# Ten projection slabs formed by token and turned by transposes, and the first half's end moved behind the second half's inverses

## The chip, the cores and the metric

The kernel runs on one core of one Trainium2 chip, as one launch. The metric is the device time of that launch in microseconds (us). Three runs of the kernel before gave 1227.54, 1227.72 and 1228.52; the median is 1227.72. TensorE (PE) does the matmuls, and its weight loads are listed apart as PEld; VectorE is DVE, ScalarE is ACT, GpSimd is POOL and SyncE is SP. Each engine takes its instructions strictly in the order in which they stand in the program.

## What is computed

One decoder layer on x of 256 tokens by 2048 channels, all in float32. Cut to what matters here:

```
u = rms_norm(x) * norm1_g                       # 256 x 2048
q, k, v, z = split(u @ w_in)                    # 3 x 1024 columns, then 3360 for z
z = z + (previous token's z - z) * shift_mix
r, k7, v7, w_lo, a_lo, g_lo = split(z)          # 3 x 1024 columns, then 288
attn = 16 heads of windowed attention on q, k, v
rw   = 16 heads of a delta-rule recurrence over the 256 tokens (r, k7, v7, decay from w_lo,
       rate from a_lo), then a norm per head, a bonus, and a gate from g_lo
h   = x + concat(attn, rw) @ w_out
out = rms_norm(h + (silu(gate) * up) @ w_down), gate, up = rms_norm(h) @ w_gate_up
```

## The kernel before

Every matmul against a big weight is made of three products of two-part numbers. A weight piece is split into `wh` (ACT copies it at reduced precision, line 148) and `wl` (DVE takes the rest, line 149), the activations likewise (`u1h`, `u1l`), and each output gets high x high, high x low and low x high. Weights come by SP's queue in pieces of 512 KB, three buffers deep, and six split pieces may stand ahead of PE. So ACT and DVE work about six pieces ahead, and in their order the other work stands between pieces.

The layer is worked in this order. A start normalises x and forms the 288 narrow columns (`lo`). Then `projections` goes through two halves of 512 channels (8 heads each), and in each half through six slabs of 512 columns: k7, r, v7 (tiles `zk`, `zr`, `zv`), then v, q, k of attention (`v`, `qT`, `kT`). Then come the product with w_out (slabs `p` and `o`), the two FFN products (`ga`, `gb`, `up`, then `d`), and the final norm.

Two ways of forming a slab exist. `slab` makes it by token: the tokens are the stationary operand, the weights stream through, 512 columns an instruction, 6 instructions for each of 16 chunks of the inner dimension. `slab_T` makes it by channel: the weights are stationary and the 256 tokens stream through, so an instruction has 256 columns, and a slab takes two passes with 96 instructions each. In the kernel before only v goes by `slab` in the projections; the other five of each half go by `slab_T`, since the later steps want channels on the partitions. The token's normalising factor then lies along the free axis, so it is laid out once over all partitions as `rbc1` (`along_tokens`, lines 263 to 270), and DVE multiplies every 128x256 block by it (lines 483 and 923).

Beside these main slabs runs side work: the recurrence of a half and its attention. It is written as generators that `run` and `step` (lines 203 to 233) mix in: after each piece of a main slab up to two side steps are issued if their due time has come, in units of a simple clock (`now`), and a generator that yields "wait" is passed over. That alone sets the order of the side instructions; nothing is reordered by time on the chip.

For each half the recurrence needs the inverse of a triangular 64x64 block per head and chunk. Its 32x32 corners (`T1`, lines 726 to 740) are found by 31 dependent steps on DVE. Then T1 and a rearranged copy of it (`U1`, a copy by ACT, line 757, in the buffer `e9`) go to DRAM and come back in another layout as `T` and `U64` (lines 755 to 771, all DMAs on ACT's queue). PE then forms the missing corner with `T` (`C0h`), then with `U64` (`C1h`), line 775 on. The recurrence proper follows (`Zh`, `Xh`, `Hh`, `Yh`), and its output `y` also lies in `e9`. At the end of a half (`end`, lines 863 to 903) y is normalised, turned by eight transposes (`tyh`, line 892), scaled and gated into `mix`. The first half's `end` runs as soon as the second half has passed `products.add` (line 725), which is ahead of the second half's 31 steps. `U1` of the second half has to wait until the first half's `y` in the same buffer is read.

The product with w_out takes four groups of channels in the order `OORD`: groups 0 and 1 are attention of the two halves, groups 2 and 3 the recurrence of the two halves. The first two groups in that order are needed by slabs `p` and `o` right after the projections.

Of the kernel before, what the change touches and what calls it, by code (L numbers as in the profile page):

```python
# [16 lines left out]
P = 128  # L17
SEQ = 256
# [57 lines left out]
def layer(ctx: ExitStack, tc: tile.TileContext, I, out, dbg=None, upto=99):  # L76
# [27 lines left out]
    rstd2 = const.tile([P, 2], F32, tag="rstd2", name="rstd2")  # L104
    rstd3 = const.tile([P, 2], F32, tag="rstd3", name="rstd3")
    mhalf = const.tile([P, 2], F32, tag="mhalf", name="mhalf")
    rbc1 = const.tile([P, SEQ], F32, tag="rbc1", name="rbc1")
    DVE.memset(mhalf, -0.5)
    DVE.memset(eps[:, 0:1], GN_EPS)
    DVE.memset(eps[:, 1:2], 1e-24)  # L110
# [42 lines left out]
    def plan_slab(w_ap, kcs, col, n, keep=None):  # L153
        g = 4 if n == 256 else 2
        for g0 in range(0, len(kcs), g):
            plan.append((w_ap, kcs[g0:g0 + g], col, n, keep))

    def take(w_ap, kc, col, units=1):
        key = (w_ap.tensor.name, kc, col)
        while wq[0] < len(plan) and (key not in made or wq[0] * 2 < wq[1] + AHEAD):  # L160
            make(wq[0])
            wq[0] += 1
        wq[1] += units
        return made.pop(key)
# [4 lines left out]
    def slab(ps, w_ap, kcs, col, n, lhs, begin=True, end=True, held=None, tokens=(0, 1)):  # L169

        for i, kc in enumerate(kcs):
# [7 lines left out]
                PE.matmul(o, ah[:, sl], lo[:, :n], start=False, stop=False)  # L179
                PE.matmul(o, al[:, sl], hi[:, :n], start=False, stop=fin)  # L180
            yield

    def slab_T(ps, w_ap, col):

        for kc in range(NK):
            hi, lo = take(w_ap, kc, col, 0.5)
            uh_, ul_ = ulhs(kc)
            for b in range(2):
                cb = slice(b * P, (b + 1) * P)
                o = ps[b][:, 0:SEQ]  # L190
                PE.matmul(o, hi[:, cb], uh_, start=kc == 0, stop=False)  # L191
                PE.matmul(o, hi[:, cb], ul_, start=False, stop=False)  # L192
                PE.matmul(o, lo[:, cb], uh_, start=False, stop=kc == NK - 1)  # L193
            if kc % 2:
                yield

# [124 lines left out]
    for half in range(2):  # L323
        for blks in ((4, 3, 5), (2, 0, 1)):
            for blk in blks:
                col = blk * AW + half * 512
                for c in (col,) if blk == 2 else (col, col + 256):
                    plan_slab(w_in, allk, c, 512 if blk == 2 else 256)
    grp = lambda gs: [k for g in gs for k in range(4 * g, 4 * g + 4)]
    for sl in (2, 3, 0, 1):  # L330
        plan_slab(w_out, grp(OORD[:2]), sl * 512, 512)
# [22 lines left out]
    with tc.tile_pool(name="startp", bufs=1) as st:  # L354
# [57 lines left out]
                ACT.activation(sqj, x_sb[:, t, q * 512:(q + 1) * 512], AF.Square, accum_out=acc[:, t, q:q + 1])  # L412
        DVE.tensor_reduce(accs1, acc, axis=AX.X, op=ALU.add)
        rms_scale(rstd1, accs1)
        along_tokens(rbc1, rstd1, st)
        for t in range(2):

            z = st.tile([P, 480], F32, tag="zlo", name=f"zlo{t}", bufs=2)
# [45 lines left out]

    rp = head_pools.enter_context(tc.tile_pool(name="rp", bufs=1, reuse_waits="tile"))

    def rwkv(half):
        hb = half * 4
        H = f"h{half}"

        def e(i, name, dt=F32):
            return rp.tile([P, 4, SEQ], dt, tag=f"e{i}", name=f"{name}_{H}")

        Z = {}

        def zin(pool, tag, which, name):
            dst = pool.tile([P, 4, SEQ], F32, tag=tag, name=f"{name}_{H}")
            for q in range(2):
                ps = banks(f"{name}{H}{q}")
                yield from slab_T(ps, w_in, RB + which * RW + half * 512 + q * 256)  # L480
                for j in range(2):
                    z = zp.tile([P, SEQ], F32, tag="ztok", name=f"z_{name}{H}{q}{j}", bufs=2)
                    DVE.tensor_tensor(z, ps[j][:, 0:SEQ], rbc1, op=ALU.mult)
                    c = which * 8 + hb + 2 * q + j
                    shift_mix(dst[:, 2 * q + j, :], z, P, V_MIX + c, c)
            Z[name] = dst

        def inputs():
            tags = ((rp, "e2"), (rp, "e1"), (rp, "e3")) if half == 0 else ((act_p, "mx3"), (act_p, "mx1"), (rp, "zvb"))
            for (pool, tag), (which, name) in zip(tags, ((1, "zk"), (0, "zr"), (2, "zv"))):  # L490
                yield from zin(pool, tag, which, name)

        return inputs, rwkv_side(half, hb, H, e, Z)

    def rwkv_side(half, hb, H, e, Z):
# [120 lines left out]
        def core():  # L616
# [97 lines left out]
            for cp in range(2):  # L714
# [7 lines left out]
                    nu = flat(e(6, "nu"))  # L722
                    ACT.dma_start(nu, d1.rearrange("u (s t) -> u s t", t=32))
                yield
            products.add(half)
            T1 = flat(e(3, "T1"))
            POOL.memset(T1, 0.0)
            POOL.memset(T1.rearrange("p a b -> p (a b)")[:, 0::33], 1.0)
# [5 lines left out]
            for t in range(31):  # L734
                a, b = 31 - t, t + 1
                w = tmp[:, 0:a * b].rearrange("p (a b) -> p a b", b=b)
                DVE.tensor_tensor(w, bc(nu[:, t, t + 1:32].unsqueeze(2), [HD, a, b]),
                                  bc(T1[:, t, 0:b].unsqueeze(1), [HD, a, b]), op=ALU.mult)
                DVE.tensor_tensor(T1[:, t + 1:32, 0:b], T1[:, t + 1:32, 0:b], w, op=ALU.add)
                if t % 3 == 2:  # L740
                    yield SUB
                if t == 17:

                    for cp in range(2):
                        pt = opsum(f"AV{H}{cp}")
                        for h in range(8):
                            for c2 in range(2):
                                kr = half_of(1 - c2)
                                PE.matmul(pt[half_of(c2), h * HD:(h + 1) * HD], abk[kr, 2 * cp + c2, h, 0:HD],
                                          vv[cp][kr, c2, h, :], start=True, stop=True,  # L750
                                          tile_position=(64 * (1 - c2), 64 * c2))
                        ACT.copy(av[:, 8 * cp:8 * cp + 8, :], pt.rearrange("p (u i) -> p u i", i=HD))
                    yield
            yield LAT[1]
            ACT.dma_start(d2[0], T1.rearrange("p s t -> p (s t)"))
            U1 = flat(e(9, "U1"))
# [106 lines left out]
        def end():  # L863
            y, bonus = Z["y"], Z["bonus"]
            if half == 1:
                yield from need("gate")
            else:
                while 1 not in products:
                    yield "wait"

            for cp in range(2):
# [35 lines left out]
    def att_inputs(half, Z):  # L907
        A = f"b{half}"
        for i, nm in ((2, "v"), (0, "qT"), (1, "kT")):
            col = i * AW + half * 512  # L910
            if nm == "v":
                ps = banks(f"v{A}")
                yield from slab(ps, w_in, allk, col, 512, ulhs)
                z = Z[nm] = zp.tile([P, 2, 512], F32, tag="atv", name=f"v{A}")
                for t in range(2):
                    ACT.activation(z[:, t, :], ps[t], AF.Copy, scale=rstd1[:, t:t + 1])
            else:
                z = Z[nm] = rp.tile([P, 4, SEQ], F32, tag=nm, name=f"{nm}{A}")
                for q in range(2):
                    ps = banks(f"{nm}{A}{q}")  # L920
                    yield from slab_T(ps, w_in, col + q * 256)
                    for j in range(2):
                        DVE.tensor_tensor(z[:, 2 * q + j, :], ps[j][:, 0:SEQ], rbc1, op=ALU.mult)

    def attention(quad, Z):

        A = f"a{quad}"
        v, qT, kT = Z["v"], Z["qT"], Z["kT"]
        h0 = quad * 4
        bias = rp.tile([P, 4, 256], F32, tag="bias", name=f"bias{A}")  # L930
# [96 lines left out]
            DVE.tensor_tensor(ml[g][:, o, :], mixt[g][:, o, :], mh[g][:, o, :].bitcast(F32), op=ALU.subtract)  # L1027

    mlhs = pair(mh, ml)
    rw, at, done, products = [], [], set(), set()  # L1030
    run(projections())


# [165 lines left out]
KEEP = 8  # L1199
LAT = (6, 5, 2, 6, 5, 3)  # L1200
BS = 1.0
WARM = 8
SUB = 1.5
SIDE_US, MAIN_US, DELAY, EL = 0.9, 1.3, 0.5, 1.5
OORD = (2, 0, 3, 1)


# [22 lines left out]
```

## Time and profile before

| what | value |
|---|---|
| median of three runs | 1227.72 us |
| the profiled execution | 1225.73 us, its span 1224.0 us |
| PE busy | 1204.0 us, 98% of the span |
| DVE busy | 819.0 us, 67% |
| ACT busy | 693.6 us, 57% |
| start | 0 to 29 us |
| projections, ten `slab_T` and two `slab` | 29 to 364 us |
| product with w_out | 369 to 486 us |
| FFN and the rest | 486 to 1224 us |

The span runs from the first instruction to the last; the execution's time has 1.7 us more around it. A matmul's row in the trace is longer than its turn on PE, since matmuls overlap: what a matmul costs is the distance from its start to the next one's start. An idle time in brackets at a row's end says how long the engine waited and for whom.

### The profile page before, as it was taken

What the parts mean: (1) busy time and instruction counts of PE and PEld (TensorE: products, weight loads), DVE (VectorE), ACT (ScalarE), POOL (GpSimd) and SP (SyncE); (2) the same over time, 40 slices, a digit from 0 to 9 for tenths busy, and PEclk for the clock granted to TensorE, in tenths of its full rate; (3) what the DMA queues carried; (4) which work ended last, traced back from release to release, by engine and by line L of the source; (5) the groups of instructions that cost most, each with busy time, mean ns of one, the idle gap of its engine ahead of it and who ended that gap; (6) DMA issues with size and microseconds to landing.
All of it is one profiled execution on the core that took longest, in us unless ns stands there. A gap on an engine that the chain in (4) does not pass through costs nothing.

```text
span 1224.0 us, 21228 instructions
## 1 busy us (share of the span) xinstructions
PE 1204.0 (98%) x7932; PEld 1057.0 (86%) x7932; DVE 819.0 (67%) x1563; ACT 693.6 (57%) x1332; POOL 39.5 (3%) x64
## 2 busy tenths in 40 slices
PE   8999999999999999999999999999999999999997
PEld 7999998898997788888888888888888888888885
DVE  5887786697877757666667566576566655565653
ACT  7875556674557556555555555565555545454543
POOL 4000000000100000000000000000000000010100
PEclk9999999999999999999999999999999999999999
DMA  8656565356674467666666666666666666666664
GB/s 245 197 167 187 155 193 161 96 167 170 177 193 139 132 175 224 201 193 189 190 190 190 190 189 190 190 189 190 189 190 190 192 195 190 195 190 199 184 202 138
DMA packets 148472, 224.05 MB, mean 183 GB/s; under 512 B 18396, under 2 KB 65760, under 8 KB 148368
## 3 DMA queue, kind: packets, MB, share of 16 engines
q1 hardware_dynamic: 132176, 211.12, 58.6%
q10 hardware_dynamic: 13920, 6.06, 1.9%
q0 software_dynamic: 2272, 5.50, 1.4%
q8 instruction: 62, 1.02, 0.4%
q14 instruction: 42, 0.34, 0.1%
HBM read 218.96 MB, written 3.69 MB: 182 GB/s over the span
## 4 chain that ended last, share of the span: by engine, by line
PE 94%; DMA 2%; ACT 1%; DVE 1%; issue 1%; SPq 0%; POOLq 0%; POOL 0%; ACTq 0%; DVEq 0%
PE up L1107 13%; PE ga L1107 7%; PE gb L1107 7%; PE up L1108 7%; PE d L180 6%; PE d L179 6%; PE d L178 6%; PE gb L1108 3%; PE ga L1108 3%; PE o L179 2%; PE o L180 2%; PE o L178 2%; PE qTb L191 1%; PE vb L178 1%; PE zvh L193 1%; PE zvh L192 1%
## 5 line engine op out<-in xcount | busy, mean ns | idle before, releaser
L149 DVE TENSOR_TENSOR wl<-wr,wh 128x512 fp32r<-128x512 f32 (+1 forms) x792 | 541.8, 691 | 346.7 <-ACT wh L148 329.8
L148 ACT ACTIVATE wh<-wr 128x512 fp32r<-128x512 f32 (+1 forms) x792 | 492.5, 627 | 460.4 <-DVE wl L149 245.6
L1107 PE MATMUL up<-u,wh 128*128 128x512 f32 x704 | 244.6, 394 | 0.0
L1108 PE MATMUL up<-u,wl 128*128 128x256 f32 x704 | 195.0, 277 | 0.0
L1107 PEld LDWEIGHTS up<-u,wh 128*128 128x128 f32 x704 | 132.0, 188 | 30.7
L1108 PEld LDWEIGHTS up<-u,wl 128*128 128x128 f32 x704 | 132.1, 188 | 0.0
L178 PE MATMUL d<-wh,hh 128*128 128x512 f32 x336 | 130.7, 389 | 0.0
L180 PE MATMUL d<-wh,hl 128*128 128x512 f32 x336 | 130.7, 389 | 0.0
L179 PE MATMUL d<-wl,hh 128*128 128x512 f32 x336 | 130.7, 389 | 0.0
L1107 PE MATMUL gb<-u,wh 128*128 128x512 f32 x352 | 130.1, 394 | 0.0
L1107 PE MATMUL ga<-u,wh 128*128 128x512 f32 x352 | 129.9, 393 | 0.0
L1108 PE MATMUL gb<-u,wl 128*128 128x256 f32 x352 | 97.6, 277 | 0.0
L1108 PE MATMUL ga<-u,wl 128*128 128x256 f32 x352 | 97.6, 277 | 0.0
L1107 PEld LDWEIGHTS ga<-u,wh 128*128 128x128 f32 x352 | 66.0, 187 | 15.3
L1107 PEld LDWEIGHTS gb<-u,wh 128*128 128x128 f32 x352 | 66.0, 187 | 15.2
L179 PEld LDWEIGHTS d<-wl,hh 128*128 128x128 f32 x336 | 63.1, 188 | 13.2
L178 PEld LDWEIGHTS d<-wh,hh 128*128 128x128 f32 x336 | 63.1, 188 | 13.1
L180 PEld LDWEIGHTS d<-wh,hl 128*128 128x128 f32 x336 | 63.1, 188 | 13.0
L1108 PEld LDWEIGHTS ga<-u,wl 128*128 128x128 f32 x352 | 66.1, 188 | 0.1
L1108 PEld LDWEIGHTS gb<-u,wl 128*128 128x128 f32 x352 | 66.1, 188 | 0.0
L178 PE MATMUL o<-wh,mixh 128*128 128x512 f32 x96 | 37.7, 393 | 0.0
L179 PE MATMUL o<-wl,mixh 128*128 128x512 f32 x96 | 37.6, 391 | 0.0
(340 smaller groups left out, 2050.3 us busy)
## 6 DMA issues: line engine op xcount, KB each, us to landing
wr<-in_w_gate_up_dram SPq DMA_DIRECT2D x176, 512.0 KB, 3.7
wr<-in_w_in_dram SPq DMA_DIRECT2D x96, 512.0 KB, 3.8
wr<-in_w_down_dram SPq DMA_DIRECT2D x88, 512.0 KB, 4.5
wr<-in_w_out_dram SPq DMA_DIRECT2D x32, 512.0 KB, 3.9
wr<-in_w_in_dram SPq DMA_DIRECT2D x8, 288.0 KB, 5.2
x_sb<-in_x_dram SPq DMA_DIRECT2D x8, 256.0 KB, 6.8
biasa<-rvd ACTq DMA_DIRECT2D x4, 512.0 KB, 4.0
xs<-in_x_dram POOLq DMA_DIRECT2D x4, 512.0 KB, 5.5
```

The lines of the kernel that those rows point to most:

```text
L148: ACT.activation(hi[:, :, :n], src, AF.Copy)
L149: DVE.tensor_tensor(lo[:, :, :n], src, hi[:, :, :n].bitcast(F32), op=ALU.subtract)
L178: PE.matmul(o, ah[:, sl], hi[:, :n], start=first, stop=False)
L179: PE.matmul(o, ah[:, sl], lo[:, :n], start=False, stop=False)
L180: PE.matmul(o, al[:, sl], hi[:, :n], start=False, stop=fin)
L191: PE.matmul(o, hi[:, cb], uh_, start=kc == 0, stop=False)
L192: PE.matmul(o, hi[:, cb], ul_, start=False, stop=False)
L193: PE.matmul(o, lo[:, cb], uh_, start=False, stop=kc == NK - 1)
L1107: PE.matmul(ps[b], hi[:, cb], u, start=kc == 0, stop=False)
L1108: PE.matmul(ps[b][:, 0:SEQ], lo[:, cb], u[:, 0, :], start=False, stop=kc == NK - 1)
```

## The change

Three things. First, the five `slab_T` slabs of each half are formed by token too, as `v` is: 96 instructions of 512 columns. ACT copies both token halves out of PSUM with the token's factor as its per-partition scale (new function `by_channel`), so `rbc1` and the DVE multiplies go. A side generator `turn`, due 1.5 units of the clock later, turns the slab by eight 128x128 transposes in two groups of four. For r, k7 and v7 the shift mix then reads the turned block in PSUM as it read the DVE product before; for q and k ACT copies it to SBUF. Attention waits until `kT` is there. Second, the first half's `end` waits for the second half's inverse steps to be done (`solved`, set after line 753) and no longer only for its products. Third, `OORD` is (0, 2, 3, 1) in place of (2, 0, 3, 1), so that slab `p` begins with group 0. Weight pieces of 256 columns no longer occur; the bytes loaded are the same.

```diff
-    rbc1 = const.tile([P, SEQ], F32, tag="rbc1", name="rbc1")
...
-    def slab_T(ps, w_ap, col):
...
-                for c in (col,) if blk == 2 else (col, col + 256):
-                    plan_slab(w_in, allk, c, 512 if blk == 2 else 256)
+                plan_slab(w_in, allk, col, 512)
...
-        along_tokens(rbc1, rstd1, st)
...
+    def by_channel(name, col, use, end):
+        ps = banks(name)
+        yield from slab(ps, w_in, allk, col, 512, ulhs)
+        z = zp.tile([P, 2, 512], F32, tag="ztok", name=f"zt_{name}")
+        for t in range(2):
+            ACT.activation(z[:, t, :], ps[t], AF.Copy, scale=rstd1[:, t:t + 1])
+
+        def turn():
+            yield TURN
+            for q in range(2):
+                pt = opsum(f"zt{name}{q}")
+                for j in range(2):
+                    for t in range(2):
+                        c = (2 * q + j) * P
+                        PE.transpose(pt[:, j * 256 + t * P:j * 256 + (t + 1) * P], z[:, t, c:c + P], ident)
+                use(q, pt)
+                if q == 1:
+                    end()
+                yield
+        side.append(turn())
...
-            for q in range(2):
-                ps = banks(f"{name}{H}{q}")
-                yield from slab_T(ps, w_in, RB + which * RW + half * 512 + q * 256)
+            def use(q, pt):
                 for j in range(2):
-                    z = zp.tile([P, SEQ], F32, tag="ztok", name=f"z_{name}{H}{q}{j}", bufs=2)
-                    DVE.tensor_tensor(z, ps[j][:, 0:SEQ], rbc1, op=ALU.mult)
                     c = which * 8 + hb + 2 * q + j
-                    shift_mix(dst[:, 2 * q + j, :], z, P, V_MIX + c, c)
-            Z[name] = dst
+                    shift_mix(dst[:, 2 * q + j, :], pt[:, j * 256:(j + 1) * 256], P, V_MIX + c, c)
+            yield from by_channel(f"{name}{H}", RB + which * RW + half * 512, use, lambda: Z.update({name: dst}))
...
-            products.add(half)
...
+            solved.add(half)
             yield LAT[1]
             ACT.dma_start(d2[0], T1.rearrange("p s t -> p (s t)"))
...
-                while 1 not in products:
+                while 1 not in solved:
                     yield "wait"
...
-                        DVE.tensor_tensor(z[:, 2 * q + j, :], ps[j][:, 0:SEQ], rbc1, op=ALU.mult)
+                def use(q, pt, z=z):
+                    ACT.copy(z[:, 2 * q:2 * q + 2, :].rearrange("p a t -> p (a t)"), pt)
+                yield from by_channel(f"{nm}{A}", col, use, lambda nm=nm, z=z: Z.update({nm: z}))
...
+        while "kT" not in Z:
+            yield "wait"
...
-OORD = (2, 0, 3, 1)
+OORD = (0, 2, 3, 1)
```

The order in which the instructions stand, at three places. On PE, in the second half, around the end of the slab `zr` (tiles `zrh`) and the start of `zv` (`zvh`); before:

```order
L191 MATMUL zrh_1_3456<-u1h_91,wh_1_3469 128x256
L192 MATMUL zrh_1_3456<-u1l_95,wh_1_3469 128x256
L193 MATMUL zrh_1_3456<-u1h_91,wl_1_3470 128x256
L191 MATMUL zvh_0_3628<-u1h_88,wh_0_3513 128x256
L192 MATMUL zvh_0_3628<-u1l_92,wh_0_3513 128x256
L193 MATMUL zvh_0_3628<-u1h_88,wl_0_3514 128x256
L191 MATMUL zvh_1_3629<-u1h_88,wh_0_3513 128x256
```

After, from the tenth matmul of `zv` on (`ztzrh` are the transposes of the copied slab `zt_zrh`):

```order
L177 MATMUL zvh_1_2953<-wh_1_2887,u1h_87 128x512
L178 MATMUL zvh_1_2953<-wl_1_2888,u1h_87 128x512
L179 MATMUL zvh_1_2953<-wh_1_2887,u1l_91 128x512
L466 MATMUL ztzrh_2981<-ident,zt_zrh_2948 128x128 x4
L177 MATMUL zvh_0_2952<-wh_0_2909,u1h_87 128x512
L178 MATMUL zvh_0_2952<-wl_0_2910,u1h_87 128x512
L179 MATMUL zvh_0_2952<-wh_0_2909,u1l_91 128x512
L177 MATMUL zvh_1_2953<-wh_0_2909,u1h_87 128x512
L178 MATMUL zvh_1_2953<-wl_0_2910,u1h_87 128x512
L179 MATMUL zvh_1_2953<-wh_0_2909,u1l_91 128x512
L466 MATMUL ztzrh_3001<-ident,zt_zrh_2948 128x128 x4
```

Where two passes ran into the next slab without a break, two groups of four transposes now stand in the next slab, the first of them 12 matmuls after the slab's end.

On ACT, in the second half, where T1 is done and goes through DRAM (`d2h`); before:

```order
L755 DMA d2h_4030<-T_h_4217 64x1024
L148 ACTIVATE wh_1_4741<-wr_4735 128x512
L757 COPY U_h_4798<-T_h_4217 64x1024
L148 ACTIVATE wh_0_4771<-wr_4769 128x512
L758 DMA d2h_4030<-U_h_4798 64x1024
L148 ACTIVATE wh_1_4775<-wr_4769 128x512
L148 ACTIVATE wh_0_4813<-wr_4811 128x512
L770 DMA T_h_4895<-d2h_4030 32x16x32
L148 ACTIVATE wh_1_4817<-wr_4811 128x512
L148 ACTIVATE wh_0_4847<-wr_4845 128x512
L771 DMA U_h_4896<-d2h_4030 32x16x32
```

After, from the last pieces made ahead of the end of slab `kT` (`zt_kTb` is its copy; line 457 makes it, 762 is U1's copy, 776 loads U64):

```order
L147 ACTIVATE wh_0_3988<-wr_3986 128x512
L457 ACTIVATE zt_kTb_4019<-kTb_0_3713,rstd_79 128x512
L147 ACTIVATE wh_1_3992<-wr_3986 128x512
L762 COPY U_h_3950<-T_h_3520 64x1024
L457 ACTIVATE zt_kTb_4019<-kTb_1_3714,rstd_79 128x512
L763 DMA d2h_3327<-U_h_3950 64x1024
L926 COPY kTb_3712<-ztkTb_4032 128x512
L1033 ACTIVATE mixh_4038<-mix_1112 128x512 x2
L926 COPY kTb_3712<-ztkTb_4052 128x512
L776 DMA U_h_4010<-d2h_3327 32x16x32 x4
L147 ACTIVATE wh_0_4085<-wr_4083 128x512
```

The store of T1 and the two loads of `T` still stand some ten pieces ahead of this place; the copy of U1, its store and the four loads of `U64` now stand behind the end of slab `kT`, with one of the slab's two copies behind U1's.

On PE, at the same place, the end of the last slab of the projections and the first matmuls of `p`; before:

```order
L192 MATMUL kTb_1_4804<-u1l_95,wh_1_4817 128x256
L193 MATMUL kTb_1_4804<-u1h_91,wl_1_4818 128x256
L943 MATMUL Sa_4978<-kTb_4650,qTb_4249 128x128
L943 MATMUL Sa_4979<-kTb_4650,qTb_4249 128x128
L943 MATMUL Sa_4978<-kTb_4650,qTb_4249 128x256
L943 MATMUL Sa_4979<-kTb_4650,qTb_4249 128x256
L943 MATMUL Sa_4988<-kTb_4650,qTb_4249 128x128
L943 MATMUL Sa_4989<-kTb_4650,qTb_4249 128x128
L943 MATMUL Sa_4988<-kTb_4650,qTb_4249 128x256
L943 MATMUL Sa_4989<-kTb_4650,qTb_4249 128x256
L780 MATMUL C0h_4998<-T_h_4895,abkh_4028 32x32 x32
L178 MATMUL p_0_4965<-wh_0_4847,mixh_4953 128x512
```

After:

```order
L178 MATMUL kTb_1_3714<-wl_1_3894,u1h_90 128x512
L179 MATMUL kTb_1_3714<-wh_1_3893,u1l_94 128x512
L897 MATMUL tyh_4002<-ident,y_h_2336 128x128 x4
L466 MATMUL ztkTb_4032<-ident,zt_kTb_4019 128x128
L177 MATMUL p_0_4044<-wh_0_3919,mixh_4022 128x512
L178 MATMUL p_0_4044<-wl_0_3920,mixh_4022 128x512
L179 MATMUL p_0_4044<-wh_0_3919,mixl_4023 128x512
L177 MATMUL p_1_4045<-wh_0_3919,mixh_4022 128x512
L178 MATMUL p_1_4045<-wl_0_3920,mixh_4022 128x512
L179 MATMUL p_1_4045<-wh_0_3919,mixl_4023 128x512
L466 MATMUL ztkTb_4052<-ident,zt_kTb_4019 128x128
L177 MATMUL p_0_4044<-wh_1_3923,mixh_4022 128x512
```

The first half's transposes `tyh`, which stood inside the slab `qT` before, now stand right here; the slab's own transposes follow, with six matmuls of `p` between; the attention scores (`Sa`) and `C0h`, which followed the slab directly, come after another twelve instructions.

## Rows read from the trace of the kernel before


**Rows 1.** The page, busy time of each engine (busy us, share of span, instructions).

```profile
PE 1204.0 (98%) x7932; PEld 1057.0 (86%) x7932; DVE 819.0 (67%) x1563; ACT 693.6 (57%) x1332; POOL 39.5 (3%) x64
```

**Rows 2.** The page, the chain that ended last, shares of the span by engine.

```profile
PE 94%; DMA 2%; ACT 1%; DVE 1%; issue 1%; SPq 0%; POOLq 0%; POOL 0%; ACTq 0%; DVEq 0%
```

**Rows 3.** Waits of PE in 40 to 364 us (total, times, longest).

```profile
PE bsh L564 <- DVE blh L560: 1.1, 2, 1.0
```

**Rows 4.** Windows: PE, PEld, DVE, ACT, POOL busy, granted clock, DMA share, GB/s.

```profile
260.00:280.00 20.00, 20.00 (x169) 20.00 (x168) 19.98 (x47) 13.56 (x23) 1.11 (x2) 1.00 0.65 185
```

**Rows 5.** Timeline of PE (start, length), 256 columns: first and last of 116 matmuls.

```profile
349.81 0.28 PE L192 MATMUL kTb<-u1l,wh 128*128 128x256 f32 x1
...
363.61 0.28 PE L193 MATMUL kTb<-u1h,wl 128*128 128x256 f32 x1
```

**Rows 6.** Timeline of PE, 512 columns: first and last of 18 matmuls.

```profile
440.04 0.39 PE L178 MATMUL o<-wh,mixh 128*128 128x512 f32 x1
...
443.90 0.39 PE L180 MATMUL o<-wh,mixl 128*128 128x512 f32 x1
```

**Rows 7.** Timeline of PE, four transposes inside a slab of 512 columns.

```profile
128.84 0.39 PE L180 MATMUL vb<-wh,u1l 128*128 128x512 f32 x1
129.07 0.60 PE L711 MATMUL tbh<-ident,bk_h 128*128 128x128 f32 x4
129.42 0.48 PE L178 MATMUL vb<-wh,u1h 128*128 128x512 f32 x1
129.74 0.39 PE L179 MATMUL vb<-wl,u1h 128*128 128x512 f32 x1
...
130.67 0.39 PE L180 MATMUL vb<-wh,u1l 128*128 128x512 f32 x1
```

**Rows 8.** Timeline of PE, first matmuls of a 512-column slab: first and fifth.

```profile
284.50 0.40 PE L178 MATMUL vb<-wh,u1h 128*128 128x512 f32 x1
...
285.43 0.39 PE L179 MATMUL vb<-wl,u1h 128*128 128x512 f32 x1
```

**Rows 9.** Timeline of PE, a 256-column slab going on after transposes.

```profile
136.74 0.36 PE L191 MATMUL qTb<-u1h,wh 128*128 128x256 f32 x1
136.94 0.28 PE L192 MATMUL qTb<-u1l,wh 128*128 128x256 f32 x1
```

**Rows 10.** Timeline of PE, laying out the factor along the tokens, at the start.

```profile
28.35 0.61 PE L269 MATMUL rbc<-ident,rb 128*128 128x128 f32 x4
```

**Rows 11.** Timeline of PE, the wait for `blh` in the first half.

```profile
73.47 0.50 PE L564 MATMUL bsh<-blh,onesblk 128*128 128x512 f32 x1 [0.97 <-DVE blh L560]
```

**Rows 12.** ACT by line and form (busy us, mean ns, idle before, releasers).

```profile
L916 ACT ACTIVATE vb<-vb,rstd 128x512 f32<-128x512 f32 x4 | 2.7, 685 | 0.1
L629 ACT ACTIVATE pw_h<-sc_h 128x1024 f32<-128x1024 f32 x2 | 2.1, 1060 | 2.6 <-DVE sc_h L623 2.6
```

**Rows 13.** Timeline of PE, from the last slab of the projections into `p`.

```profile
363.82 1.58 PE L943 MATMUL Sa<-kTb,qTb 64*128 64x128 f32 x16
367.98 1.20 PE L780 MATMUL C0h<-T_h,abkh 32*32 32x32 f32 x64 [2.58 <-DMA T_h<-d2h]
```

**Rows 14.** Timeline of ACT and its DMA issues (ACTq), the way through DRAM.

```profile
352.43 2.09 ACT L757 COPY U_h<-T_h 64x1024 f32<-64x1024 f32 x1
354.55 0.45 ACTq L758 DMA_DIRECT2D d2h<-U_h  x1
...
359.42 0.31 ACTq L771 DMA_DIRECT2D U_h<-d2h  x1
361.86 0.31 ACTq L770 DMA_DIRECT2D T_h<-d2h  x1
```

**Rows 15.** Timeline, the second half's `end`, on PE and DVE.

```profile
412.84 0.69 PE L813 MATMUL Yh<-vv_h,abkh 128*64 128x64 f32 x16
...
417.88 0.69 DVE L884 TENSOR_TENSOR y_h<-y_h,rsh 128x512 f32<-128x512 f32 x1
...
420.17 0.60 PE L892 MATMUL tyh<-ident,y_h 128*128 128x128 f32 x4
```

More of the change, by code (lines that the diff above doesn't have):

```diff
@@ L181, in slab @@
             yield
-    def slab_T(ps, w_ap, col):
[L185 to L195, printed above, removed]
     side, ready, now = [], {}, [0.0]
@@ L917, in att_inputs @@
             else:
[L918 to L922, printed above, removed]
-                        DVE.tensor_tensor(z[:, 2 * q + j, :], ps[j][:, 0:SEQ], rbc1, op=ALU.mult)
+                z = rp.tile([P, 4, SEQ], F32, tag=nm, name=f"{nm}{A}")
+                def use(q, pt, z=z):
+                    ACT.copy(z[:, 2 * q:2 * q + 2, :].rearrange("p a t -> p (a t)"), pt)
+                yield from by_channel(f"{nm}{A}", col, use, lambda nm=nm, z=z: Z.update({nm: z}))
     def attention(quad, Z):
         A = f"a{quad}"
+        while "kT" not in Z:
+            yield "wait"
         v, qT, kT = Z["v"], Z["qT"], Z["kT"]
@@ L1029, in layer @@
     mlhs = pair(mh, ml)
-    rw, at, done, products = [], [], set(), set()
+    rw, at, done, solved = [], [], set(), set()
     run(projections())
@@ L1201 @@
 BS = 1.0
+TURN = 1.5
 WARM = 8
```

## The prediction, made before the changed kernel ran

> **What bounds the kernel now.** First the page's busy times, then its chain: PE is busy for 98% of the span [rows 1], and the chain that ended last runs through PE for 94% of it, no other engine for more than 2% [rows 2]. The reader is to see that a microsecond counts only if PE gains or loses it. Next the waits of PE in the projections: they come to about 1 us [rows 3]. Then the window in which DVE has most to do: DVE is busy for 19.98 of 20 us and PE still for all 20 [rows 4], so the six pieces made ahead carry PE over a full DVE. The granted clock is 1.00 there, the upper of the two levels; the page shows tenths of 9 throughout, so I expect no clock effect. What remains is to count what PE issues, from start to start, and to look at the few places where it waits.
>
> **The change part by part.** The sum is made against the profiled execution, 1225.73 us, span 1224.0; the median is 1227.72, 2.0 above it. The sum is then set on the median.
>
> *Ten slabs by token.* The 116 matmuls of 256 columns from 349.81 to 363.61 have 115 distances in 13.80 us, 120.0 ns each [rows 5]. The 18 of 512 columns from 440.04 to 443.90 have 17 in 3.86 us, 227 ns each [rows 6]; I use 226.7. A slab by channel is 192 x 0.1200 = 23.04 us, by token 96 x 0.2267 = 21.76. So 1.28 a slab, ten slabs: -12.8 us.
>
> By the Trainium skill, page "TensorE: Matmul & The Clock Gate", section "Back-to-back issue gap", a matmul by itself takes its columns over 2.4 plus 2.5 ns, so two of 256 would cost only 2.5 ns more than one of 512; 960 fewer instructions would then give 2.4 us in place of 12.8. The same section says that in a stream weight loads share in the spacing. The trace disagrees with the first rule here: 2 x 120.0 - 226.7 = 13.3 ns.
>
> *Transposes.* Each of the ten slabs adds two groups of four. In the slab `v` such a group stands between 128.84 and 130.67, with six matmuls: 1.83 us [rows 7]. Six matmuls alone are 1.36, so a group costs 0.47, which includes the slower first matmul behind it. Twenty groups: +9.4. If only the rise of that first matmul is shared with side work that stands at the same place, a group is 0.44, and twenty are 8.8: the lower bound.
>
> *Breaks.* Behind any other work the first matmul of 512 columns takes 0.32 (129.42 to 129.74), 0.09 above its pitch [rows 7], and the next ones are slow too: four distances from 284.50 to 285.43 are 0.2325 each [rows 8], so six such give 0.035 more. A break costs 0.125. With 256 columns the first takes 0.20 (136.74 to 136.94) against 0.12, and nothing after [rows 9]: 0.08. Before, some 39 groups of side work break the ten slabs; 39 x 0.045 = 1.75 if all stay apart, 0 if all fall together with transposes. I take +0.7.
>
> *The factor along the tokens.* Four matmuls of 0.61 in all at the start go [rows 10]; some of it overlaps, so -0.5.
>
> *First half's wait for `blh`.* PE waits 0.97 for DVE [rows 11], 1.1 with a second [rows 3]. DVE's chain to `blh` begins after the slab `zr`; that use now comes twelve matmuls later, while the DVE product ahead of it goes. The wait can stay whole (0) or go (-1.1). I take -0.6.
>
> *`zr` of the second half.* By the order the first transposes stand 12 matmuls, 2.7 us, behind the slab's end. On ACT the first copy (0.685, the row of the same form for v), an exponent of 1.06 [rows 12], two splits (0.63 each from their busy time over count) and the second copy stand in that span: 3.3 to 3.7 us. A wait of 0.6, between 0 and 1.
>
> *ACT and DVE.* ACT gains 20 copies of 0.685 [rows 12] and 8 of q and k; DVE loses 40 multiplies and reads the shift mix out of PSUM. I cost both at nothing: PE's six pieces ahead hide them. With that cover gone each slab's two copies would show, 1.4 us.
>
> *End of the second half.* Before, the scores `Sa` start at 363.82, and `C0h` then waits 2.58 us for `T` to land [rows 13]. Now T1's store and `T`'s loads stand ten pieces earlier, so this wait goes. What is late next: U1's copy, 2.09 us [rows 14], cannot start before `tyh` has freed its buffer, and it stands between ACT's two copies of `kT`. So the first transposes wait about 0.9 and `Sa` about 0.2. Then ACT stands at `U64`'s loads until U1's store has landed; before, issue of that store to first load behind it was 354.55 to 359.42, 4.87 us [rows 14]. The softmax exponents queue behind this on ACT, and `PTa` and `Oa` on PE wait for them: 0.7 and 0.5, since some 45 matmuls of `p` (10 us) stand ahead of them. Together 2.3 in place of 2.58: -0.3. With no wait at all it would be -2.6; with all of 4.87 and 2.09 seen by PE, +4.4.
>
> *First half.* The same `C0h` of the first half stands a little nearer to its load: +0.2 (0 to 0.6).
>
> *Tail.* `Yh` at 412.84, y normalised at 417.88 + 0.69, transposes at 420.17 [rows 15]: the chain needs 5.7 us and had 7.3. By the new order only 3.8 chunks of six matmuls with what lies between, 6.1 us, stand between `Yh` and `tyh`: +0.3 for a wait behind DVE's splits (0 to 1).
>
> Nothing is added to SP's queue: fewer, larger pieces, the same bytes.
>
> Sum: -12.8 + 9.4 + 0.7 - 0.5 - 0.6 + 0.6 - 0.3 + 0.3 + 0.2 = -3.0. So 1222.7 for the profiled execution, 1224.7 for the median.
>
> **The rivals.**
>
> *R1, slower: the way of U1 through DRAM ends behind its use.* `C1h` of the second half needs `U64`. From the slab's end: `tyh`, U1's copy (2.09), the store (4.87), then four loads in a row; `T`'s load, issued at 361.86, lands just before 367.98, 6.1 us [rows 13, 14]. With queueing on ACT about 15.5 us. By the order some fifty matmuls of 512 columns (11.3 us), the small side work and the waits above stand ahead of `C1h`, about 20 us. If each of the two DMAs takes twice as long, it ends at 26.5 and PE, strict in its order, stands at `C1h` for 6.5 us: -3.0 + 6.5 = +3.5, 1231.2. It decides from 20 us on. For it: ACT's queue is in order, and all of this moved behind the slab's end. Against: rows of the same transfers, with 4.5 us to spare.
>
> *R2, no gain: the 512-column pitch never settles.* With transposes, score blocks and copies breaking every slab, the matmuls stay at the 0.2325 of [rows 8]. A slab is then 22.32, saving 0.72, ten -7.2 in place of -12.8; against it 0.035 a break is already in it, about 1.5: -3.0 + 5.6 - 1.5 = +1.1, 1228.8. For it: in the first nine matmuls of `v` it is so. Against: a long stretch settles to 0.227 [rows 6], and a slab has some 70 matmuls between breaks.
>
> *R3, larger gain: the waits go.* All of the 1.1 at `blh`, all of the 2.58 at `C0h`, transposes at 0.44, no breaks added, no new waits: -12.8 + 8.8 - 0.5 - 1.1 - 2.6 = -8.2, 1219.5. For it: each is the favourable end of a bound. Against: it needs all of them.
>
> *R4, slower: one instruction of 512 columns takes nearly as long as two of 256.* The 227 ns are read in the product with w_out. If in the ten slabs the distance were 0.2375, a slab would take 22.80 and save 0.24, ten 2.4: -3.0 + 10.4 = +7.4, 1235.1. Against it: `v` runs in the projections, and even its first distances are 0.2325 [rows 8]. The Trainium skill's rule for a single matmul, told above, comes to the same.
>
> **How the numbers follow.** What can be told from no change is 0.2%, 2.5 us: faster is under 1225.3, slower over 1230.2. The forecast has 0.44; its own range, from the ends of the small terms, is 1222.5 to 1227, of which 0.28 is faster, 0.16 the same. R3 0.14, all faster. R2 0.20: 0.05 faster, 0.13 same, 0.02 slower. R1 0.19: 0.01 same, 0.18 slower. R4 0.03 slower. Together faster 0.47, same 0.30, slower 0.23. The range leaves out R4, the upper part of R1 and the lower end of R3, about 2 in 10: 1219.8 to 1230.4.
>
> **What would show it.** Right: in a slab such as `kT` distances of 0.227 in the stretches, about 21.8 us and 0.9 for its transposes; a period of 1.83 with four transposes in it; no wait at `C0h` for `T`; instead waits of under 1 us at the transposes of `kT`, at `PTa` and at `Oa`, for ACT. Wrong: a granted clock under 1.0 in the projections; a wait at `C1h` for `U64` (R1); distances of 0.2325 throughout (R2); a gap in the slab behind the second half's `zr` of more than 1 us; or PE waiting for `wl` or `wh`, which would mean that the cover of six pieces doesn't hold.

## The result, and the profile after

The changed kernel takes 1222.38 us (median of 5 runs, 1221.81 to 1223.28) against 1228.0 of the kernel before beside it (5 runs, 1227.54 to 1231.28). The ratio is 0.995, 95% interval 0.9938 to 0.9962: 5.6 us less, between 4.7 and 7.6. The forecast was 3.0 less.

The two profiled executions are only 2.8 apart (1225.73 and 1222.94, spans 1224.0 and 1221.2). So half of what was timed does not stand between these two traces; where it is, the experiments below had to find. The page's busy times and the chain's shares of the changed kernel, which answer to [rows 1, 2]:

```profile
PE 1203.2 (99%) x7048; PEld 1013.3 (83%) x7048; DVE 805.9 (66%) x1521; ACT 710.4 (58%) x1361; POOL 39.5 (3%) x64
...
PE 90%; ACT 4%; DMA 2%; issue 1%; DVE 1%; ACTq 0%; SPq 0%; POOL 0%; POOLq 0%; DVEq 0%
```

PE is still the bound. ACT's share of the chain has risen from 1 to 4%: the chain passes over to ACT where PE now waits for its copies, but the waits themselves come to under 4 us. PE's waits (total, times, longest), from 26 us on:

```profile
PE ztzkh L466 <- ACT zt_zkh L457: 1.8, 2, 1.0
PE ztkTb L466 <- ACT zt_kTb L457: 1.0, 1, 1.0
PE Oa L984 <- ACT pTa L977: 0.5, 1, 0.5
PE PTa L976 <- DVE sa L968: 0.4, 1, 0.4
PE ztzrh L466 <- ACT zt_zrh L457: 0.2, 1, 0.2
PE bsh L568 <- ACT bhh L564: 0.2, 1, 0.2
```

The wait of 1.1 for `blh` [rows 3, 11] has become 0.2, that of 2.58 at `C0h` [rows 13] is gone, and so are two of 0.7 each, in the kernel before:

```profile
PE C1h L782 <- DVE sa L949: 0.7, 1, 0.7
PE ptlo L453 <- ACT rbc L270: 0.7, 1, 0.7
```

The first is that of the first half. The second stood at the transposes of `lo`, which had waited for the factor laid along the tokens (the kernel with the slabs alone, below, still has 0.7 there for another copy, so that this one is not sure to be the change's).

A stretch of the slab `kT` of the changed kernel on PE: 27 matmuls, 26 distances in 5.90 us, 226.9 ns each, as in [rows 6]:

```profile
349.86 0.39 PE L177 MATMUL kTb<-wh,u1h 128*128 128x512 f32 x1
...
355.76 0.39 PE L179 MATMUL kTb<-wh,u1l 128*128 128x512 f32 x1
```

And a group of four transposes in the slab behind `zr`, six matmuls with it in 1.82 us (84.03 to 85.85), as in [rows 7]:

```profile
84.03 0.39 PE L179 MATMUL zvh<-wh,u1l 128*128 128x512 f32 x1
84.26 0.60 PE L466 MATMUL ztzrh<-ident,zt_zrh 128*128 128x128 f32 x4
84.62 0.47 PE L177 MATMUL zvh<-wh,u1h 128*128 128x512 f32 x1
...
85.85 0.40 PE L179 MATMUL zvh<-wh,u1l 128*128 128x512 f32 x1
```

The end of the second half on PE, which answers to [rows 13]:

```profile
363.30 0.87 PE L466 MATMUL ztkTb<-ident,zt_kTb 128*128 128x128 f32 x6 [1.01 <-ACT zt_kTb L457]
...
365.48 1.58 PE L950 MATMUL Sa<-kTb,qTb 64*128 64x128 f32 x16
367.11 1.20 PE L785 MATMUL C0h<-T_h,abkh 32*32 32x32 f32 x64
...
376.87 0.33 PE L976 MATMUL PTa<-ident,sa 128*128 128x128 f32 x1 [0.40 <-DVE sa L968]
...
378.76 0.87 PE L984 MATMUL Oa<-pTa,vb 128*64 128x256 f32 x8 [0.49 <-ACT pTa L977]
379.56 1.20 PE L787 MATMUL C1h<-U_h,T_h 32*32 32x32 f32 x64
```

`C0h` follows `Sa` without a wait; small waits stand at the three places that the prediction named (that of `PTa` is for DVE, where the prediction had ACT); `C1h`, 19.7 us behind the slab's end, does not wait for `U64`.

### The profile page after: what moved, and what is told of

It is laid out like the page before. It is cut to its first block, busy times and chain, and to the rows that moved or that the text cites. A ratio compares the mean times of both kernels' runs of the same rounds, so it can differ in the third digit from the quotient of the medians.

```text
span 1221.2 us, 19390 instructions
## 1 busy us (share of the span) xinstructions
PE 1203.2 (99%) x7048; PEld 1013.3 (83%) x7048; DVE 805.9 (66%) x1521; ACT 710.4 (58%) x1361; POOL 39.5 (3%) x64
## 4 chain that ended last, share of the span: by engine, by line
PE 90%; ACT 4%; DMA 2%; issue 1%; DVE 1%; ACTq 0%; SPq 0%; POOL 0%; POOLq 0%; DVEq 0%
PE up L1114 13%; PE gb L1114 7%; PE ga L1114 7%; PE up L1115 7%; PE d L177 6%; PE d L178 6%; PE d L179 6%; PE gb L1115 3%; PE ga L1115 3%; PE o L177 2%; PE o L178 2%; PE o L179 2%; PE vb L177 1%; PE kTb L177 1%; PE vb L179 1%; PE vb L178 1%
```

## The experiments

Each was timed beside runs of the kernel before, whose medians there were 1228.46 to 1228.49; the ratios are to these.

**The kernel before once more.** No edit.

> The kernel before, unchanged, for a second profile. The timed difference (1228.0 to 1222.4, -5.6) is twice that of the two profiled executions (1225.73 to 1222.94, -2.8). Theory A: the runs of before differ at the DMAs on which PE waits, T's landing at C0h (2.58 us in the first profile) above all; a profile of 1227.5 or more would show a wait of 4 us or more there. Rival B: they differ at the start, where x lands (1.7 us for pt_u in the first profile), and then the wait at C0h stays at 2.6. Rival C: neither differs, and the first profile was simply quick. Time 1227 to 1229 under each.

1227.52, ratio 0.9997 (0.9988 to 1.0006). Its profile is of an execution of 1229.43, 3.7 above the first. On PE, and in windows (PE, PEld, DVE, ACT, POOL busy, granted clock, DMA share, GB/s):

```profile
369.94 1.20 PE L780 MATMUL C0h<-T_h,abkh 32*32 32x32 f32 x64 [3.22 <-DMA T_h<-d2h]
371.07 0.79 PE L178 MATMUL p<-wh,mixh 128*128 128x512 f32 x1
```

```profile
24.00:28.00 4.00, 4.00 (x17) 4.00 (x18) 3.81 (x11) 3.83 (x11) 1.62 (x3) 0.50 0.72 213
370.00:374.00 4.00, 4.00 (x71) 3.38 (x72) 2.51 (x5) 1.16 (x2) 0.00 (x0) 0.63 0.49 145
374.00:378.00 4.00, 4.00 (x17) 3.25 (x17) 2.42 (x3) 3.25 (x13) 0.00 (x0) 0.94 0.00 0
```

The wait for T is 3.2, not 4 or more. But behind it the granted clock is 0.63 and 0.94 of full speed in two windows of 4 us, that is 2.4 GHz with a part at 1.2, and the first matmul of `p` takes 0.79 where it took 0.50: 4 x 0.37 + 4 x 0.06 = 1.7 us lost. The rows agree: from the first to the ninth matmul of `p` it is 3.50 us (371.07 to 374.57) where it was 1.94 (369.11 to 371.05). The first trace of before has 1.00 there:

```profile
370.00:374.00 4.00, 4.00 (x20) 3.29 (x18) 3.60 (x5) 3.18 (x12) 0.00 (x0) 1.00 0.38 123
```

Also at the start, behind PE's wait for the last pieces of `lo`, the clock is 0.50 in this execution and was 1.00 in the first. The changed kernel shows that one too, and full speed behind the projections:

```profile
24.00:28.00 4.00, 4.00 (x19) 3.45 (x17) 4.00 (x15) 3.46 (x8) 1.82 (x3) 0.62 0.90 280
...
370.00:374.00 4.00, 4.00 (x19) 3.34 (x18) 1.66 (x3) 3.68 (x11) 0.00 (x0) 1.00 0.36 64
```

So neither A nor B as written: the executions of before differ by the wait, by the clock behind it and by the start. The trace that I predicted from was one with the clock up at both places; it lost speed at a third, earlier one:

```profile
8.00:12.00 4.00, 4.00 (x22) 3.92 (x20) 2.83 (x7) 3.56 (x12) 3.04 (x7) 0.57 1.10 341
```

**The pause filled.** In the kernel before, ahead of the second half's `C0h`:

```diff
+                if half == 1 and step_ == 0:
+                    for _ in range(22):
+                        PE.matmul(pt[:, 0:SEQ], onesblk, ulhs(0)[0], start=True, stop=True)
```

> The kernel before, with 22 idle matmuls of 256 columns (22 x 0.12 = 2.6 us, their result overwritten) ahead of the second half's C0h, where PE waited 2.6 and 3.2 us for T in two profiles. In the second of them the granted clock was 0.63 in 370 to 374 us, behind the wait, in the first 1.00. Theory A (the pause costs twice: its own length, and in most executions a lower clock behind it): C0h waits under 1 us behind the filling, the clock stays 1.00 in 366 to 378 and the time falls by 1.5 to 2, to 1226 to 1227. Rival B (the pause costs its length alone, the clock there is chance): no change, 1227.5 to 1228.5.

1226.96, ratio 0.9987 (0.9979 to 0.9996): A. PE works through but for 0.2 us, on PE and in the windows:

```profile
365.61 2.36 PE L779 MATMUL C0h<-u1h,onesblk 128*128 128x256 f32 x18
...
368.74 0.63 PE L779 MATMUL C0h<-u1h,onesblk 128*128 128x256 f32 x4
...
370.25 1.20 PE L783 MATMUL C0h<-T_h,abkh 32*32 32x32 f32 x64
```

```profile
370.00:374.00 4.00, 4.00 (x77) 3.26 (x76) 3.27 (x6) 3.10 (x7) 0.00 (x0) 1.00 0.45 134
```

With matmuls that compute nothing the kernel is 1.5 us faster, close to the 1.7 read from the clock. The edit did one thing more: in the order that came of it six matmuls of `p` stand among the idle ones, ahead of `C0h`. They are not where the gain is. From the start of `Sa` to the first matmul of `p` behind `C0h` it is 7.40 us here (363.98 to 371.38), 6.0 without these six, against 5.93 in the second trace of before (365.14 to 371.07) and 5.29 in the first: the filled stretch is no shorter, and what is gained lies behind it, at full speed. Its twelve runs also lie closer together (1226.0 to 1227.5) than the eleven of the unchanged kernel (1226.2 to 1229.4).

**The order without the slabs.** The kernel before with `solved` and `OORD`:

```diff
-            products.add(half)
...
+            solved.add(half)
...
-                while 1 not in products:
+                while 1 not in solved:
...
-OORD = (2, 0, 3, 1)
+OORD = (0, 2, 3, 1)
```

> The kernel before with only the second and third part of the change: the first half's end waits for the second half's steps, and the order of the groups is (0, 2, 3, 1). Slabs stay by channel. Theory A (the ten slabs with their transposes give -3, the waits little): T's loads come earlier and the wait of 2.6 at C0h goes, waits of about 1.2 at PTa and Oa come, so -1 to -2, 1226 to 1227. Rival B (the gain is the order's, the slabs give nothing): -4 to -6, 1222 to 1224. Rival C (order alone exposes U1's way): 1229 or more, with a wait at C1h.

1228.42, ratio 0.9998 (0.9986 to 1.0011). T's loads do come earlier, but a wait stays:

```profile
370.35 1.20 PE L780 MATMUL C0h<-T_h,abkh 32*32 32x32 f32 x64 [2.41 <-DVE sa L949]
```

PE now waits for DVE, which has the first half's end to do at this place and behind it the multiplies of `kT` and the reading of `Sa`. One wait took the place of another, and the clock is 0.81 and 0.76 in the 8 us from 370 on: none of A, B and C.

**The slabs without the order.** The changed kernel with the reverse of the edit above.

> The changed kernel with the first half's end again behind products alone and the order of groups again (2, 0, 3, 1): only the ten slabs by token with their transposes. Theory A: slabs and transposes -3, the waits at the start (ptlo, 0.7) and for blh (0.9) gone, 1.8 at the first transposes of zk added, T's wait at C0h still there, 2 to 3 us: -3 to -4.5, 1223.5 to 1225. Rival B (all in the order): 1227.5 to 1228.5.

1228.88, ratio 1.001 (0.9999 to 1.002): the rival's time within 0.4, but not for its reason. In its trace `kT` ends at 360.3, 3.4 us earlier than in the first trace of before, and then PE stands:

```profile
366.89 1.92 PE L785 MATMUL C0h<-T_h,abkh 32*32 32x32 f32 x64 [6.42 <-DMA T_h<-d2h]
```

```profile
366.00:370.00 4.00, 3.11 (x70) 3.08 (x71) 0.78 (x2) 1.15 (x2) 0.00 (x0) 0.50 0.67 147
370.00:374.00 4.00, 4.00 (x18) 3.31 (x17) 1.07 (x2) 2.11 (x5) 0.00 (x0) 0.86 0.00 0
```

T lands when the chain through DVE's 31 steps and DRAM has it, at 366.9 against 368.0 and 369.9 in the two traces of before. What PE saves ahead of it is waited away at `C0h`, with the clock down behind.

**Only the order of groups, with the slabs by channel.** `OORD` alone in the kernel before.

> The kernel before with only the order of groups (0, 2, 3, 1). PE's instructions stand in the same order as before, C0h ahead of every matmul of p; only which mix p reads first differs. With the slabs by token the same edit gave -5.7 (1228.88 to 1223.23), with 24 matmuls of p ahead of C0h in its order. Theory A (the gain comes from matmuls of p that stand ahead of C0h while T is on its way): nothing here, 1227.5 to 1229, and a wait of 2.5 us or more at C0h. Rival B (p on group 0 is ready sooner, wherever it stands): 1223 to 1225.

1228.98, ratio 1.001 (0.9992 to 1.0027), and in PE's waits

```profile
PE C0h L780 <- DMA T_h<-d2h: 3.3, 1, 3.3
```

A: nothing without work that stands ahead of `C0h`.

**Slabs and order of groups, the end early.** In the changed kernel:

```diff
+            solved.add(half)
             T1 = flat(e(3, "T1"))
...
-            solved.add(half)
             yield LAT[1]
```

> The changed kernel, with the first half's end let go again as soon as the second half's products stand; the order of groups stays (0, 2, 3, 1). Theory A (the end's work ahead of the 31 steps is what makes T late): C0h waits over 4 us for T as with the slabs alone (6.4), the time is 1227 to 1229. Rival B (the order of groups is what matters): 1222 to 1223.

1223.23, ratio 0.9961 (0.9948 to 0.9973): B, 0.2 above its range. The wait for T is there, but later and without a fall of the clock:

```profile
361.30 0.39 PE L177 MATMUL p<-wh,mixh 128*128 128x512 f32 x1
...
366.51 0.39 PE L179 MATMUL p<-wh,mixl 128*128 128x512 f32 x1
369.55 1.20 PE L785 MATMUL C0h<-T_h,abkh 32*32 32x32 f32 x64 [2.65 <-DMA T_h<-d2h]
```

24 matmuls of `p` on group 0 stand between the slab and `C0h` and start without a wait, 5.4 us that PE spent waiting in the kernel with the slabs alone. The 5.7 between these two kernels, which differ in the order of groups only, are 3.8 of wait (6.42 and 2.65) and 1.7 of clock: from the start of `C0h` to the third matmul of `p` behind it is 4.25 us there (366.89 to 371.14) and 2.53 here (369.55 to 372.08). The later end, which is all that is left to the changed kernel, brings 0.9 by the medians, which these runs don't separate from nothing.

**Slabs and the later end, the old order of groups.** `OORD` back in the changed kernel.

> The changed kernel with the order of groups again (2, 0, 3, 1). Theory A (the first half's end now runs at the end of the last slab, so a p that begins with group 2 comes too early for it): PE waits 3 to 6 us for mix at the start of p, 1226 to 1229. Rival B (the order of groups is of no account, the mix is ready in time): 1222 to 1223.

1227.77, ratio 0.9993 (0.9985 to 1.0002): A by the time. But PE doesn't wait at the start of `p` for mix; it waits ahead of it, at the transposes of `kT`, for ACT's copy:

```profile
363.84 1.54 PE L466 MATMUL ztkTb<-ident,zt_kTb 128*128 128x128 f32 x6 [2.50 <-ACT zt_kTb L457]
365.42 1.64 PE L950 MATMUL Sa<-kTb,qTb 64*128 64x128 f32 x6
366.99 0.79 PE L177 MATMUL p<-wh,mixh 128*128 128x512 f32 x1
```

```profile
366.00:370.00 4.00, 4.00 (x13) 2.31 (x10) 1.75 (x4) 0.89 (x2) 0.18 (x1) 0.50 0.76 177
```

`p` on group 2 can't fill the gap, since that group's mix is only being made; PE pauses at the transposes, and `p` starts with the clock down again (0.79).

Put together:

| slabs | groups | first half's end | us |
|---|---|---|---|
| channel | 2, 0, 3, 1 | early | 1227.5 to 1228.5 (before) |
| channel | 0, 2, 3, 1 | early | 1228.98 |
| channel | 0, 2, 3, 1 | late | 1228.42 |
| token | 2, 0, 3, 1 | early | 1228.88 |
| token | 2, 0, 3, 1 | late | 1227.77 |
| token | 0, 2, 3, 1 | early | 1223.23 |
| token | 0, 2, 3, 1 | late | 1222.38 (after) |

Of the eight kernels that these three parts make, one was not run: slabs by channel, the old order of groups, the late end. What is gained, is gained where slabs by token and the new order of groups come together: 5.7 with the early end, 5.4 with the late one.

The granted clock of each run, a mean over its span, is on record too. It doesn't tell the place, but it sorts the kernels. Of the 88 runs of the kernel before that were made for these experiments (two at 1317 and 4214 us left out) 29 have 0.996 or more, with a median of 1227.4 us, and 59 have 0.995 or less, with 1228.7. Of the filled kernel's runs all twelve have 0.996 or more, of the changed kernel's all five, with the early end five of six; with the slabs alone none of eleven, with the old order of groups one of twelve.

**The transposes twice.**

```diff
-                for j in range(2):
-                    for t in range(2):
+                for j, t in 2 * [(j, t) for j in range(2) for t in range(2)]:
```

> The changed kernel with each group of four transposes issued twice into the same place: 80 transposes more in groups that are there already. Theory A (a group costs 0.35 for its four turns and 0.12 for the break behind it, and the break is paid once): 20 x 0.35 = +7.0, 1229.4. Rival B (each group of four costs its 0.47 whole): +9.4, 1231.8. Rival C (the transposes lie in time in which PE would wait anyway): under +4, 1226 or less.

1230.34, by the medians 8.0 above the changed kernel; ratio to before 1.0019 (1.001 to 1.0028): between A and B. A group of eight on PE:

```profile
86.92 1.04 PE L465 MATMUL ztzrh<-ident,zt_zrh 128*128 128x128 f32 x8
87.71 0.47 PE L177 MATMUL zvh<-wh,u1h 128*128 128x512 f32 x1
```

0.79 for eight, 0.36 for four: the second four cost 0.43, twenty times 8.6, of which 8.0 are seen (7.5 if each kernel is taken against the runs of before beside it). The transposes are nearly all on PE's path.

**The transposes a piece later.** `TURN` 3.0 for 1.5.

> The changed kernel with TURN = 3.0 for 1.5: each slab's transposes stand a piece (six matmuls) later. Theory A (the waits of 1.8 us at zk's first transposes, of 1.0 at kT's and of 0.2 at zr's are ACT being late, and nothing behind them is short of time): these waits go, 1219.3 to 1220.5. Rival B (the later use only moves the waits to Sa, PTa and what follows zk): 1221.5 to 1223.

1226.11, 1223.87 to 1238.18, ratio 1.0006 (0.9982 to 1.003; five of the twelve runs took 1228.9 or more, which the ratio counts and the median doesn't): neither theory. At the first half's `zk` the edit moved nothing, twelve matmuls of `zr` stand ahead of the transposes as before, and the 1.8 there stays; behind the other slabs they stand later. One new wait comes in the second half:

```profile
260.90 0.50 PE L178 MATMUL zvh<-wl,u1h 128*128 128x512 f32 x1 [3.06 <-DVE wl L148]
```

DVE, in its order, stood 3.7 us for ACT ahead of this split: the six pieces' cover ran out. Why single runs go up to 1238 I did not follow.

**zk's copies on DVE.**

```diff
+            if (name, t) in ON_DVE:
+                DVE.tensor_scalar(z[:, t, :], ps[t], rstd1[:, t:t + 1], None, op0=ALU.mult)
+            else:
+                ACT.activation(z[:, t, :], ps[t], AF.Copy, scale=rstd1[:, t:t + 1])
...
+ON_DVE = {("zkh0", 0), ("zkh0", 1)}
```

> The changed kernel with DVE in place of ACT for the two copies of the first half's zk. In the trace of after these two stand on ACT behind an exponent of 1.05, a table load of 1.28 and two splits, and PE waits 1.8 us for them. Theory A (ACT late is the whole of it): the wait goes, 1220.3 to 1221.3. Rival B (DVE is as late, or the splits on DVE are held up): 1222 or more.

1224.88, ratio 0.9962 (0.9948 to 0.9976): B, DVE is later still.

```profile
PE ztzkh L469 <- DVE zt_zkh L458: 2.8, 1, 2.8
```

**And the second half of kT's.** `("kTb1", 1)` added to `ON_DVE`.

> As the run before, and the second half of the second kT's copy also on DVE, so that U1's copy of 2.08 us on ACT no longer stands between slab and transposes. Theory A: the wait of 1.0 at kT's transposes goes as well, 1219.5 to 1220.5. Rival B (DVE is busy with the first half's end there; kT's copy, or the mix, gets later): no better than the run before, or 1 us worse.

1224.14, ratio 0.9963 (0.995 to 0.9976): the wait of 1.0 at `kT`'s transposes is gone, but waits of 0.8 and 0.4 at `Sa` are new and zk's is 2.1: B.

**The start filled.** As the first of these two, and in `lo`, ahead of its last piece of the third group:

```diff
+            fill = opsum("fill")
+            for _ in range(10):
+                last = PE.matmul(fill, wz[:, 0:P], wz, start=True, stop=True)
...
```

> As g2, and ten idle matmuls of 512 columns in the start, seven of them where PE waits 2.1 us for the last weight pieces of lo at 20.4 us. In the profile of after the clock is 0.62 in 24 to 28 us behind this wait and a matmul of 288 columns takes 0.24 in place of 0.13 for about 2.9 us: 1.3 lost. Theory A (the pause lowers the clock there too): clock 1.00 in 24 to 28, and 0.5 to 1.3 less than g2, the three other idle matmuls (0.7) set off against it. Rival B: no change, or slower by up to 0.7.

1223.44, ratio 0.9967 (0.9955 to 0.9979): inconclusive. The clock falls a little later in its profile (0.82 and 0.76 in 24 to 32 us) behind a pause that was left. None of the four tries beats the changed kernel.

## Why the prediction was right, and where its sum was off

The likeliest case held, and the time lies in the range, but the sum of -3.0 is 2.6 short. By the steps, forecast and measured:

| step | forecast | measured |
|---|---|---|
| ten slabs, twenty groups, breaks | -2.7 | -3.9 |
| factor along the tokens | -0.5 | -1.1 |
| `blh` | -0.6 | -0.9 |
| `zr` of the second half | +0.6 | +0.2 |
| ACT's copies, cover of six pieces | 0 | +1.8 |
| end of the second half, waits | -0.3 | -0.7 |
| first half behind `kT` | +0.2 | -0.5 |
| tail | +0.3 | 0 |
| PE's other work up to the FFN | 0 | +2.0 |
| clock behind the pause at `C0h` | 0 | -1.7 |
| sum | -3.0 | -4.8 |

The lines are worked out from all of PE's rows, as distances from start to start with the waits taken out: the ten slabs' matmuls fall from 235.4 to 223.3 us, the transposes take 8.2. The waits are differences of the two tables of PE's waits. The line of the other work, which the prediction didn't have, is what remains of the whole; its largest parts are the scores (`Sa` +1.3, in other places of the order), `o` (+0.7), `Zh` (+0.6) and `Ah` (+0.5). Why they cost more I did not follow.

The whole is read from `lo`, where PE goes on after a wait that both traces have, to the first matmul of the FFN: 462.6 us in the first trace of before (23.65 to 486.30) and 460.9 in the changed kernel (22.55 to 483.48), 1.7 less. Behind that wait the changed kernel ran thirteen distances of 0.24 in place of 0.13 with the clock down, 1.4 us; without them it is 3.1 less. The two whole spans can't be set against each other in this way, since the first trace has lost speed of its own ahead of this stretch, at 8 to 12 us.

So without the clock the steps come to -3.1, where -3.0 was forecast. That they agree is luck in part: the slabs and most waits came out better than forecast, by some 4 us together, and ACT's copies and PE's other work, which both stood at nothing, took 3.8 back. With the clock it is -4.8, just inside the interval that was timed, 4.7 to 7.6 less; the other 0.8 of the 5.6 has no place in these traces and stays open.

**The mis-sized term** of what was timed is the clock: "the page shows tenths of 9 throughout, so I expect no clock effect". I read the granted clock where PE works and not behind the one place where it pauses, I read it in one execution, and the page could not show it: a slice of its row is 30.6 us long, and 9 stands for everything from 0.90 up. The first trace has its 0.57 at 8 to 12 us under a 9, and the second trace's page has a 9, too, in the slice that holds 370 to 378 us:

```profile
PEclk8999999999999999999999999999999999999998
```

In the second trace of before the pause of 3.2 us is followed by 1.7 us of lost speed, the kernel with it filled is 1.5 faster, and the changed kernel's waits at this place, none above 1.0, show 1.00. That something was missing from the traced execution stood in the numbers that I had: three runs of before at 1227.5 or more, and the profile at 1225.7.

**T's wait, and what the gain hangs on.** I let T's wait go because T1's store and `T`'s loads stand earlier behind the moved end. That was right: the store is issued at 347.77 in the changed kernel and at 353.43 with the end early, the last of the two loads of `T`

```profile
352.44 0.31 ACTq L775 DMA_DIRECT2D T_h<-d2h  x1
```

in the one and

```profile
359.88 0.75 ACTq L775 DMA_DIRECT2D T_h<-d2h  x1
```

in the other, and the wait of 2.65 is gone. Its worth was forecast as small, and it is: waits of 1.9 come in its place, where 2.3 were forecast, and by the medians the moved end gives 0.9. What the prediction had no term for is that the rest hangs on matmuls of `p` which are ready when the slab ends, since `p` begins with group 0. With the early end 24 of them stand there while T is on its way. In the changed kernel 13 stand between the slab, its transposes and `C0h`; without them, in the old order of groups, PE pauses for 2.5 us at the transposes, and 5.4 us are lost in all. Ahead of the prediction I had written that due times alone set the order of the side work; the kernels with and without `OORD` differ in nothing else, and yet the 24 stand ahead of `C0h` in one and behind it in the other, so what an instruction needs counts as well when the order is made. That the parts don't add up, each alone worth nothing, I had not among the rivals.

**zk's copies.** The step "PE's six pieces ahead hide them" forgot that the transposes themselves are queued on PE and wait for ACT. On ACT around the end of the first half's slab, which PE leaves at 52.9:

```profile
52.66 1.05 ACT L636 ACTIVATE sc_h<-sc_h 128x1024 f32<-128x1024 f32 x1
53.72 1.28 ACT L587 ACT_TABLE_LOAD   x1
55.01 1.15 ACT L147 ACTIVATE wh<-wr 128x512 fp32r<-128x512 f32 x2
56.07 0.67 ACT L457 ACTIVATE zt_zkh<-zkh,rstd 128x512 f32<-128x512 f32 x1
...
57.16 0.68 ACT L457 ACTIVATE zt_zkh<-zkh,rstd 128x512 f32<-128x512 f32 x1
```

I worked out this place for `zr` of the second half (0.6 forecast, 0.2 measured) and for its `kT`, and not for the eight other slabs.

**The rivals.** R1: `C1h` had no wait, U1's way fitted. At `kT` its copy of 2.08 us did stand between ACT's two, as forecast (1.0 for 0.9), and `PTa` and `Oa` waited 0.4 and 0.5 for 0.7 and 0.5. R2 and R4: four in five of the distances within the ten slabs are 0.227, and with the slower ones behind breaks their mean is 0.230. R3 had the waits right that went, not those that came.

## What to carry to other kernels

A pause of the bounding engine can cost more than its length: look at the granted clock in the windows behind each pause, in more than one execution, before a wait is priced. What is saved ahead of a wait on another chain is lost there, unless the order puts work that is ready in between; so a faster stage and a reordering that are each worth nothing can be worth 5.6 us together, and testing them one by one would have dropped both. An operation moved to another engine is priced by what stands ahead of it in that engine's order, at each of its places.

## What was not expected of the hardware

Behind a pause of PE of 2 to 3 us the clock went down in some executions and not in others: it was 1.00 behind 2.58 and 2.65 us of waiting (the first trace of before, the changed kernel with the early end), and 0.50 behind 2.50 (the changed kernel with the old order of groups), 0.63 behind 3.22, 0.84 and 0.73 behind 3.34 (only the order of groups), 0.50 to 0.86 behind 6.42. The length of the pause alone doesn't decide; what does, the runs don't settle.
